# Output projections: the second half reads its weights' remainders from DRAM, and its squares follow the next weights' casts

## The chip, the cores and the metric

The kernel runs on one core of one Trainium2 chip. The metric is the device time of one execution in microseconds (us), the median over several runs.

## The reference

An encoder trunk of two layers over 1024 tokens of width 1024, in float32, one sequence. Layer 0 mixes with two parallel groups of heads (latent attention and stick-breaking attention), layer 1 with chunked band attention. Each mixer ends in one output projection and a residual add, and is followed by a SwiGLU feed-forward part (FFN):

```
for layer in range(2):
    u = rms_norm(h, g_mix[layer])
    o = heads of the mixer, concatenated           # (1024, 1024)
    h = h + o @ w_out[layer]                       # the output projection
    u = rms_norm(h, g_ffn[layer])
    h = h + (silu(u @ w_gate[layer]) * (u @ w_up[layer])) @ w_down[layer]
return rms_norm(h, g_final)
```

The sum of the squares of h over the 1024 features, one per token, is what the next `rms_norm` divides by.

## The kernel before, in words

**Numbers in two parts.** Matrix products are made from float32 operands split in two rounded parts: `hi` is the cast of x, `lo` the remainder x - hi. A product is three matmuls: `hi*hi`, `hi*lo`, `lo*hi` (`mm3`, lines 290 to 292). For weights the raw tile is called `wr` in the profile, the cast `wh` (on ACT, `round_to`, line 253) and the remainder `wl` (`rest`, line 258, on POOL or DVE). Each of the three has four buffers of 128x512, which is two weights, as one weight of the output projection is two such pieces.

**The output projection** works on features by tokens: two halves of 512 tokens (`hf` 0 and 1), in each eight output tiles `m` of 128 features. `out_half` makes one half. For a tile: load the residual two tiles ahead (`ld`), take the weight (two pieces, cast and remainder), eight k-steps of three matmuls into one PSUM bank (`mm`), add the residual on DVE (line 443), write the new h to DRAM (line 444), then square it on ACT and add the square to the running sum on DVE (`square_sum`, lines 305 to 314). Every half takes all eight weights, so each weight is loaded, cast and split twice per mixer.

**The first half** (`half(0)`) is woven into the attention of the last head pair. Its remainders are made by POOL. **The second half** is `half(1, 1)`: `early` is 1, the weights are cast and split one tile ahead, and their raw pieces are loaded one tile before that. Its remainders are made by DVE. It isn't run by the mixer: the mixer returns it as a generator, and `ffn` draws its steps as `rest`. The first tile runs before, the other seven within the pinned part (line 637): there PE, ACT, DVE and POOL keep the order in which the program issues their instructions, and the profile books all of them on line 77. SyncE, which issues all DMAs, isn't pinned: its order is made by the planner, by the times at which it thinks that data and buffers are ready. Between the k-steps of the second half, `ffn` issues work of its own: the norm of the first half (`blocks0`, from the matmul with `ones` that sums `s.acc[0]` over the partitions), the casts and remainders of the normed first half, and the loads, sums, casts and remainders of the FFN's first weights (`Pair`, `arrange`).

**After the second half** the FFN's products begin (`Seven`; `z` and `o` in PSUM). After the first product comes `blocks1`: the matmul with `ones` for `s.acc[1]`, the norm of the second half and the operands made from it.

Of the kernel before, what the change touches and what calls it, by code (L numbers as in the profile page):

```python
# [10 lines left out]
F32 = mybir.dt.float32  # L11
F32R = mybir.dt.float32r
AF = mybir.ActivationFunctionType
ALU = mybir.AluOpType
AX = mybir.AxisListType

P = 128
S = 1024
D = 1024
KD = D // P  # L20
HALF = 512
# [138 lines left out]
class Trunk:  # L160
# [113 lines left out]
            self.nc.sync.dma_start(tiles[-1][:, :w], src[:, c:c + w])  # L274
        return tiles

    def weight(self, src, n=1024, eng_hi="act", eng_lo="pool", into=None, raws=None):
        parts = []
        for c in range(0, n, HALF):
            w = min(HALF, n - c)  # L280
            raw = raws[c // HALF] if raws else self.raws(src[:, c:c + w], w)[0]
            hi, lo = into[c // HALF] if into else (self.wtile(0, "h", F32R), self.wtile(0, "l", F32R))
            self.split(raw[:, :w], hi[:, :w], lo[:, :w], eng_hi, eng_lo)
            parts.append((hi, lo))
        return Weight(parts)

# [138 lines left out]
                parts[k] = hi, lo  # L425
                yield

    def out_half(self, hf, w, parts, resid, ks, s, h_d, early=0):

        o = [x[0] for x in parts], [x[1] for x in parts]  # L430
        ahead, raws, wts = [], [], []
        for m in range(KD):
            while len(ahead) < min(AHEAD, KD - m):
                ahead.append(self.load(resid(hf, m + len(ahead))))
            x, h = ahead.pop(0), self.unit()
            for n in range(m + len(wts), min(m + early + 1, KD)):
                raw = raws.pop(0) if raws else None
                wts.append(self.weight(w[n], eng_lo="dve" if early else "pool", raws=raw))
            if early and m + early + 1 < KD:
                raws.append(self.raws(w[m + early + 1]))  # L440
            ps = self.bank()
            yield from self.dense(ps, wts.pop(0), o, ks)
            self.nc.vector.tensor_tensor(h, ps, x, ALU.add)
            self.nc.sync.dma_start(h_d[hf][m], h)
            s.h[hf].append(h)
            s.acc[hf] = self.square_sum(s.acc[hf], h)

    def parted(self, t):

# [804 lines left out]
    def free(self, gen):  # L1254

        for _ in gen:
            yield 0.0

    def ending(self, gen):
        yield from gen  # L1260
        self.flush()

    def mixer0(self, h_d):
        nc, a = self.nc, self.a
        o_d = self.spill("o0_")
        out = Stream()
        ks = [4, 5, 6, 7, 0, 1, 2, 3]
        half = lambda hf, *e: self.out_half(hf, a["w_out0"], o_p[hf], lambda hf, m: a["x"][hf, m], ks, out, h_d, *e)
        with self.phase("mix0", MIX0_TEMPS):
            self.load_consts()  # L1270
            vts = [[] for _ in range(4)]
            proj = ([[], []], [[], []], [])
            u = self.start(vts[0:2], proj)
            vgen = lambda w, g, hf: self.values(w, u, 4, KD, 1, vts[2 * g:2 * g + 2], hf)
            raw = [[[], []], [[], []]]
            cq, ckv = Stream(), Stream()
            va = [[] for _ in range(4)]
            mla = ([[], []], [[], []])

            def prepare():  # L1280
                yield from self.mla_latent([0, 1, 2], u, raw)
                yield from self.with_max(self.mla_latent([3, 4], u, raw), self.mla_norm(0, raw, cq), 0, 4)
                for hf in range(2):
                    nc.vector.tensor_tensor(self.cs[hf], self.cs[hf], cq.r[hf], ALU.mult)
                queries = self.chain(*[self.mla_query(e, cq, mla[0][e], "f", (0, 1)) for e in range(2)])
                yield from self.with_max(queries, self.mla_norm(1, raw, ckv), 2, 2)
                yield from self.values([a["w_uv"][0]], ckv, 2, 2, 2, va, [0, 1])
                yield from self.mla_keys(0, ckv, mla[1], "f", (0, 1))
                yield from self.free(self.mla_max(0, mla))

            for p in range(4):
                nxt = ([[], []], [[], []], [])
                if p < 2:
                    vw = [a["w_vb"][2], a["w_vb"][3]]
                    fill, cost = self.chain(self.sb_project(p + 1, u, nxt), vgen(vw, 1, [p])), 31.0
                elif p == 2:
                    fill, cost = self.chain(self.sb_project(3, u, nxt), self.rope_key(u)), 31.0
                else:
                    fill, cost = prepare(), 73.0
                self.weave(self.ending(self.sb_attend(p, proj, vts[p], o_d)) if p == 3 else  # L1300
                           self.sb_attend(p, proj, vts[p], o_d), 9.24, fill, cost)
                proj = nxt
            for p in range(4):
                nxt = ([[], []], [[], []])
                first, second = (self.mla_attend(p, hf, mla, va[p], o_d) for hf in range(2))
                top = lambda hf: self.mla_max(hf, mla)
                if p < 3:
                    att = self.chain(self.with_max(first, top(1), 0), self.with_max(second, self.mla_max(0, nxt), 4))
                    fill, cost = self.mla_project(p + 1, cq, ckv, nxt), 13.0
                    if p == 2:  # L1310
                        fill, cost = self.mla_project(3, cq, ckv, nxt, "c", [0]), 8.0
                    self.weave(att, 7.0, fill, cost)
                else:
                    o_p = [[None] * KD, [None] * KD]
                    first = self.with_max(first, self.out_loads(o_d[0], 3, o_p[0]), 0)
                    second = self.with_max(second, self.out_loads(o_d[1], 3, o_p[1]), 0)
                    fill = self.chain(self.mla_project(3, cq, ckv, mla, "c", [1]), self.free(top(1)))
                    self.weave(self.ending(first), 2.5, fill, 4.0)
                    o_p[0][3] = o_d[0][3]
                    self.weave(self.ending(second), 6.5, half(0), 41.5)  # L1320
                    o_p[1][3] = o_d[1][3]
                mla = nxt
        return out, half(1, 1)

    def mixer1(self, u, h_d, h2_d):
        a = self.a
        o_d = self.spill("o1_")
        out = Stream()
        half = lambda hf, *e: self.out_half(hf, a["w_out1"], o_p[hf], lambda hf, m: h_d[hf][m], list(range(KD)), out,
                                            h2_d, *e)  # L1330
        with self.phase("band", BAND_TEMPS):
            vts = [[] for _ in range(8)]
# [10 lines left out]
            for p in range(8):  # L1343
# [17 lines left out]
                else:  # L1361
                    o_p = [[None] * KD, [None] * KD]
# [158 lines left out]
```

## Time and profile before

| | |
|---|---|
| median of 3 runs | 2534.04 us (2530.97 to 2535.76) |
| the profiled execution | 2536.2 us, span from first to last instruction 2534.4 us |
| busy: PE, DVE, ACT, POOL | 97%, 74%, 46%, 19% of the span |
| granted TensorE clock | 0.994 |
| DMA | 324.94 MB, mean 128 GB/s |
| w_out loads | 64 of 256 KB, median 3.0 us to landing |
| second half of mixer 0 and of mixer 1, about | 616 to 665 us, 1820 to 1869 us |

A row of a timeline gives start, duration, engine, line, operation, output<-inputs and count, and in brackets how long the engine stood idle before it and who ended that. A row of waits gives who waited for whom: total us, times, longest. A row of windows gives the length, and for PE, PEld (weight loads), DVE, ACT and POOL the busy us with the number of instructions, then the granted clock, the DMA engines' busy share and GB/s. "SPq" is SyncE's DMA queue. Matmuls overlap in the pipeline, so their starts tell more than their durations.

### The profile page before, as it was taken

The page shows a single profiled execution, that of the slowest core. Times are in us where ns is not written, and L with a number is a line of the kernel's source. Part 1 is how long each engine was busy: PE and PEld are TensorE (multiplying, and loading weights), DVE is VectorE, ACT ScalarE, POOL GpSimd, SP SyncE. Part 2 cuts the span into 40 slices and gives each one's busy share as a digit, 9 for nine tenths or more (in the row PEclk, how much of TensorE's full clock was granted, in tenths as well). Part 3 has the DMA queues.
Part 4 walks back from the last instruction along what each step waited for, and adds up shares of the span by engine and source line. Part 5 has one row for each costly group of instructions (what it writes and reads, how often), then busy time and mean ns, then how long its engine had stood idle before and what let it go on. Part 6 is the DMA issues. An engine that isn't in the chain of part 4 may idle for free.

```text
span 2534.4 us, 33597 instructions
## 1 busy us (share of the span) xinstructions
PE 2460.9 (97%) x11710; PEld 1934.4 (76%) x11710; DVE 1870.9 (74%) x3072; ACT 1155.3 (46%) x2004; POOL 493.7 (19%) x475
## 2 busy tenths in 40 slices
PE   9999989999999999999999999999999999999997
PEld 7776766667778888888877777776777888888886
DVE  7988796675886666677666777778688666667775
ACT  5777565443454444433253443444445443443324
POOL 0333335761000000000132333435200000000004
PEclk9999999999999999999999999999999999999999
DMA  5222102145344434576552222223633433447661
GB/s 156 55 65 65 38 22 73 51 122 178 108 137 141 146 108 142 172 259 221 205 170 69 83 84 79 76 90 106 197 119 129 145 136 113 146 160 260 217 210 71
DMA packets 182824, 324.94 MB, mean 128 GB/s; under 512 B 21376, under 2 KB 37632, under 8 KB 182656
## 3 DMA queue, kind: packets, MB, share of 16 engines
q1 hardware_dynamic: 182656, 322.81, 38.3%
q8 instruction: 92, 1.51, 0.3%
q14 instruction: 76, 0.62, 0.1%
HBM read 223.63 MB, written 84.41 MB: 122 GB/s over the span
## 4 chain that ended last, share of the span: by engine, by line
PE 71%; DVE 9%; DMA 2%; ACT 2%; issue 1%; POOL 1%; DVEq 0%; POOLq 0%; SPq 0%; ACTq 0%
PE z L77 25%; PE mm L77 12%; PE o L77 7%; PE mm L290 6%; PE mm L291 5%; PE mm L292 5%; PE o L850 3%; DVE u L77 2%; PE z L1230 1%; PE z L1231 1%; PE z L1204 1%; DVE u L313 1%; PE z L1149 1%; PE o L1114 1%; PE z L1074 1%
## 5 line engine op out<-in xcount | busy, mean ns | idle before, releaser
L77 PE MATMUL z<-u,wh 128*128 128x512 f32 x976 | 302.2, 390 | 6.5 <-DVE u L77 6.5
L77 PE MATMUL z<-u,vh 128*128 128x512 f32 x976 | 302.8, 392 | 2.2 <-DVE u L77 2.2
L290 PE MATMUL mm<-u,wh 128*128 128x512 f32 x720 | 287.7, 400 | 3.3 <-DVE u L724 1.6
L291 PE MATMUL mm<-u,wh 128*128 128x512 f32 x720 | 283.6, 394 | 1.4 <-DVE u L258 1.4
L292 PE MATMUL mm<-u,wl 128*128 128x512 f32 x720 | 283.5, 394 | 0.0
L258 POOL TENSOR_TENSOR wl<-wr,wh 128x512 fp32r<-128x512 f32 (+2 forms) x95 | 121.5, 1283 | 785.1 <-ACT wh L253 726.2
L77 PE MATMUL mm<-u,wh 128*128 128x512 f32 x720 | 223.4, 392 | 4.6 <-ACT wh L77 4.6
L77 PEld LDWEIGHTS z<-u,wh 128*128 128x128 f32 x976 | 183.1, 188 | 47.3 <-DVE u L77 9.5
L77 PEld LDWEIGHTS z<-u,vh 128*128 128x128 f32 x976 | 183.8, 189 | 42.9 <-ACT u L77 3.1
L77 PE MATMUL z<-u,vl 128*128 128x512 f32 x488 | 190.7, 391 | 0.0
L77 PE MATMUL z<-u,wl 128*128 128x512 f32 x488 | 190.0, 389 | 0.6 <-DVE wl L77 0.6
L290 PEld LDWEIGHTS mm<-u,wh 128*128 128x128 f32 x720 | 135.6, 188 | 50.8 <-issue 23.5
L77 PEld LDWEIGHTS mm<-u,wh 128*128 128x128 f32 x720 | 134.7, 188 | 35.7 <-ACT wh L77 6.9
L292 PEld LDWEIGHTS mm<-u,wl 128*128 128x128 f32 x720 | 135.5, 188 | 29.2 <-issue 1.7
L291 PEld LDWEIGHTS mm<-u,wh 128*128 128x128 f32 x720 | 135.6, 188 | 27.3 <-DVE u L258 2.0
L77 PE MATMUL mm<-u,vh 128*128 128x512 f32 x496 | 152.7, 389 | 0.0
L77 PE MATMUL mm<-u,wl 128*128 128x512 f32 x360 | 140.8, 391 | 0.8 <-DVE wl L77 0.5
L258 POOL TENSOR_TENSOR u<-wr,u 128x512 fp32r<-128x512 f32 x8 | 10.9, 1372 | 670.2 <-ACT u L253 670.2
L850 PE MATMUL o<-a,u 128*64 128x512 f32 (+3 forms) x768 | 139.2, 474 | 0.5 <-DVE f L1122 0.4
L1097 POOL TENSOR_TENSOR b<-b,a 128x512 f32<-128x512 f32 (+3 forms) x80 | 109.2, 1365 | 122.9 <-ACT a L1233 99.5
L77 ACT CAST vh<-vr 128x512 fp32r<-128x512 f32 (+1 forms) x166 | 95.9, 578 | 81.7 <-DVE vr L77 30.8
L1233 ACT ACTIVATE a<-a 128x1024 f32<-128x1024 f32 (+3 forms) x96 | 70.0, 737 | 129.7 <-DVE a L1232 128.8
(244 smaller groups left out, 5874.1 us busy)
## 6 DMA issues: line engine op xcount, KB each, us to landing
u<-f_t SPq DMA_DIRECT2D x144, 256.0 KB, 5.0
vr<-in_w_up SPq DMA_DIRECT2D x88, 256.0 KB, 4.4
wr<-in_w_gate SPq DMA_DIRECT2D x88, 256.0 KB, 3.6
f_t<-x SPq DMA_DIRECT2D x72, 256.0 KB, 2.0
wr<-in_w_out SPq DMA_DIRECT2D x64, 256.0 KB, 3.0
f_t<-e SPq DMA_DIRECT2D x54, 256.0 KB, 3.7
ld<-f SPq DMA_DIRECT2D x54, 256.0 KB, 5.0
u<-u SPq DMA_DIRECT2D x96, 128.0 KB, 2.2
```

What stands on the lines that cost most here:

```text
L77: return lambda *a, **k: self.tc.keep_in_program_order(f(*a, **k))
L258: self.eng(eng).tensor_tensor(lo, src, hi.bitcast(F32), ALU.subtract)
L290: mm(out, wh, xh, start=first, stop=False, skip_group_check=onto)
L291: mm(out, wh, xl, start=False, stop=False, skip_group_check=onto)
L292: mm(out, wl, xh, start=False, stop=last, skip_group_check=onto)
L313: self.eng(eng).tensor_tensor(acc, acc, sq, ALU.add)
L850: return self.nc.tensor.matmul(o[rh, cs], vt[j // 4][:, j % 4, rh], w[:, e, cs], start=first, stop=last)
L1074: nc.tensor.matmul(z[:, e, :n], qs[e][hf][0][0:kr, r * P:(r + 1) * P], ks[e][kh][0][0:kr, :n], start=True, stop=True)
L1097: self.eng("dve" if dest[2] else "pool").tensor_tensor(st["esum"][:, :, cs], old[:, :, cs], ex[:, :, cs], ALU.add)
L1114: return nc.tensor.matmul(den[64 * e:64 * e + 64, :], self.ones[:, 0:64], esum[:, e, :], start=True, stop=True)
L1149: mm(z[:, e, cs], kth[0:kr, bs], qh[0:kr, cs], start=True, stop=False)
L1233: nc.scalar.activation(ex[:, :, cs], ex[:, :, cs], AF.Exp)
```

## The change

In the first half, each remainder that POOL has made is also written to a DRAM tile (`w_d`, 16 tiles of 256 KB for each mixer). In the second half, `weight` still loads the raw piece and casts it on ACT, but loads the remainder from DRAM instead of having DVE subtract. Besides, in tiles 1 to 7 of the second half, the square of the tile before no longer follows its residual add: ACT's square is issued after the second k-step (behind the casts of the next weight), and DVE adds it to the sum after the fifth. The last tile is squared as before.

```diff
-    def weight(self, src, n=1024, eng_hi="act", eng_lo="pool", into=None, raws=None):
+    def weight(self, src, n=1024, eng_hi="act", eng_lo="pool", into=None, raws=None, los=None):
...
-            self.split(raw[:, :w], hi[:, :w], lo[:, :w], eng_hi, eng_lo)
+            if los:
+                self.round_to(eng_hi, hi[:, :w], raw[:, :w])
+                self.nc.sync.dma_start(lo.bitcast(F32), los[c // HALF])
+            else:
+                self.split(raw[:, :w], hi[:, :w], lo[:, :w], eng_hi, eng_lo)
...
-    def out_half(self, hf, w, parts, resid, ks, s, h_d, early=0):
+    def out_half(self, hf, w, w_d, parts, resid, ks, s, h_d, early=0):
...
+        def add_square():
+            if s.acc[hf] is None:
+                s.acc[hf] = sq
+            else:
+                self.nc.vector.tensor_tensor(s.acc[hf], s.acc[hf], sq, ALU.add)
...
-                wts.append(self.weight(w[n], eng_lo="dve" if early else "pool", raws=raw))
+                wts.append(self.weight(w[n], raws=raw, los=w_d[n] if early else None))
+                if not early:
+                    for (_, lo), d in zip(wts[-1].parts, w_d[n]):
+                        self.nc.sync.dma_start(d, lo.bitcast(F32))
...
-            yield from self.dense(ps, wts.pop(0), o, ks)
+            for k, us in enumerate(self.dense(ps, wts.pop(0), o, ks)):
+                if early and m and k == 1:
+                    sq = self.unit()
+                    self.nc.scalar.square(sq, s.h[hf][-1])
+                if early and m and k == 4:
+                    add_square()
+                yield us
...
-            s.acc[hf] = self.square_sum(s.acc[hf], h)
+            if not early or m == KD - 1:
+                s.acc[hf] = self.square_sum(s.acc[hf], h)
...
+    def remainders(self, name):
+        return [[self.dp.tile([P, HALF], F32, name=f"{name}{m}_{c}") for c in range(2)] for m in range(KD)]
```

`mixer0` and `mixer1` make the tiles (`self.remainders("w0_")`, `self.remainders("w1_")`) and pass them to `out_half`.

More of the change, by code (lines that the diff above doesn't have):

```diff
@@ L426, in out_loads @@
                 yield
-    def out_half(self, hf, w, parts, resid, ks, s, h_d, early=0):
+    def out_half(self, hf, w, w_d, parts, resid, ks, s, h_d, early=0):
         o = [x[0] for x in parts], [x[1] for x in parts]
-        ahead, raws, wts = [], [], []
+        ahead, raws, wts, sq = [], [], [], None
+        def add_square():
[3 more added lines that the diff above has]
+                self.nc.vector.tensor_tensor(s.acc[hf], s.acc[hf], sq, ALU.add)
         for m in range(KD):
@@ L1264, in mixer0 @@
         nc, a = self.nc, self.a
-        o_d = self.spill("o0_")
+        o_d, w_d = self.spill("o0_"), self.remainders("w0_")
         out = Stream()
         ks = [4, 5, 6, 7, 0, 1, 2, 3]
-        half = lambda hf, *e: self.out_half(hf, a["w_out0"], o_p[hf], lambda hf, m: a["x"][hf, m], ks, out, h_d, *e)
+        half = lambda hf, *e: self.out_half(hf, a["w_out0"], w_d, o_p[hf], lambda hf, m: a["x"][hf, m], ks, out, h_d, *e)
         with self.phase("mix0", MIX0_TEMPS):
@@ L1326, in mixer1 @@
         a = self.a
-        o_d = self.spill("o1_")
+        o_d, w_d = self.spill("o1_"), self.remainders("w1_")
         out = Stream()
-        half = lambda hf, *e: self.out_half(hf, a["w_out1"], o_p[hf], lambda hf, m: h_d[hf][m], list(range(KD)), out,
+        half = lambda hf, *e: self.out_half(hf, a["w_out1"], w_d, o_p[hf], lambda hf, m: h_d[hf][m], list(range(KD)), out,
                                             h2_d, *e)
```

## The prediction

> **What bounds the kernel now.** I read the page first, then the PE's waits in the two stretches that the change touches, then the timelines of PE, DVE, ACT and SyncE there. The page:
>
> ```profile
> span 2534.4 us, 33597 instructions
> PE 71%; DVE 9%; DMA 2%; ACT 2%; issue 1%; POOL 1%; DVEq 0%; POOLq 0%; SPq 0%; ACTq 0%
> ```
>
> PE carries the chain that ends last, so time is won only where PE waits. The change touches the output projections: their first halves (about 505 to 622 us and 1715 to 1828 us) and their second halves, which run inside the FFN's pinned order up to the matmul with `ones` (`o<-u,ones`) that sums the squares of the second half. The PE's waits in the two second halves, mixer 0 (622 to 668.6 us), then mixer 1 (1828 to 1874.4 us); columns: total us, times, longest:
>
> ```profile
> PE mm L77 <- ACT wh L77: 2.4, 3, 1.3
> PE o L77 <- DVE u L77: 0.5, 1, 0.5
> ...
> PE mm L77 <- ACT wh L77: 2.2, 2, 1.4
> PE o L77 <- DVE u L77: 1.3, 1, 1.3
> PE z L77 <- DVE wl L77: 0.6, 1, 0.6
> ```
>
> PE waits for ACT's casts of w_out and for DVE. What that costs in full is read from the starts of matmuls in PE's timeline (start us, us):
>
> ```profile
> 627.93 0.61 PE L77 MATMUL mm<-u,wh 128*128 128x512 f32 x2
> 633.37 0.62 PE L77 MATMUL mm<-u,wh 128*128 128x512 f32 x2
> ...
> 644.76 0.73 PE L77 MATMUL mm<-u,wh 128*128 128x512 f32 x2 [0.35 <-ACT wh L77]
> 652.28 0.73 PE L77 MATMUL mm<-u,wh 128*128 128x512 f32 x2 [1.34 <-ACT wh L77]
> 659.15 0.74 PE L77 MATMUL mm<-u,wh 128*128 128x512 f32 x2 [0.69 <-ACT wh L77]
> 668.56 1.12 PE L77 MATMUL o<-u,ones 128*128 128x512 f32 x2 [0.49 <-DVE u L77]
> 1832.60 0.61 PE L77 MATMUL mm<-u,wh 128*128 128x512 f32 x2
> 1874.35 1.12 PE L77 MATMUL o<-u,ones 128*128 128x512 f32 x2 [1.31 <-DVE u L77]
> ```
>
> 627.93 is the start of output tile m=2 and 633.37 that of m=3: a tile is 8 k-steps of three matmuls and takes 5.44 us undisturbed, 0.68 us a step. From m=2 to `ones` lie six tiles and the four steps of the FFN's first product: 6 x 5.44 + 4 x 0.68 = 35.36 us. They took 668.56 - 627.93 = 40.63 us and 1874.35 - 1832.60 = 41.75 us. So PE loses 5.27 us in mixer 0 and 6.39 us in mixer 1, 11.66 us together: all there is to win in these two stretches.
>
> Why ACT's casts are late is seen in one tile (m=4), DVE rows, then ACT rows:
>
> ```profile
> 642.33 0.68 DVE L77 TENSOR_TENSOR u<-mm,ld 128x512 f32<-128x512 f32 x1
> 643.71 0.69 DVE L77 TENSOR_TENSOR u<-u,u 128x512 f32<-128x512 f32 x1 [0.70 <-ACT u L77]
> 644.32 1.28 DVE L77 TENSOR_TENSOR wl<-wr,wh 128x512 fp32r<-128x512 f32 x2
> 645.52 0.74 DVE L77 SCALAR_TENSOR_TENSOR u<-u,gains,u 128x512 f32<-128x512 f32 x1
> 649.86 0.68 DVE L77 TENSOR_TENSOR u<-mm,ld 128x512 f32<-128x512 f32 x1
> 666.43 0.68 DVE L77 TENSOR_TENSOR u<-mm,ld 128x512 f32<-128x512 f32 x1
> ...
> 643.04 0.63 ACT L77 ACTIVATE u<-u 128x512 f32<-128x512 f32 x1 [1.19 <-DVE u L77]
> 643.58 1.12 ACT L77 CAST wh<-wr 128x512 fp32r<-128x512 f32 x2
> ```
>
> DVE adds the residual of m=3 at 642.33, though PE had finished that tile at the start of m=4 (633.37 + 5.44 = 638.81): DVE is 3.5 us behind. ACT's square waits for that add, the casts for m=5 stand behind the square in ACT's queue, and PE gets them at 644.76. From this add to the next (649.86) DVE takes 7.53 us, 2.09 more than PE's tile. DVE's work per tile is what bounds this stretch.
>
> **The change part by part.** (1) Removed from DVE: two remainders (`wl<-wr,wh`) a tile. Their slot runs from 644.32 to 645.52: 1.20 us. (2) Square behind the casts: DVE no longer idles for ACT's square between residual add and sum; the sum comes at k=4 and costs its slot, the idle 0.70 us goes (643.71 - 642.33 = 1.38, less a slot of 0.61 = 0.77 with its edges). Together 1.97 us: the fullest tile falls to 7.53 - 1.97 = 5.56 us against PE's 5.44. That 0.1 us is caught up in the next tile: the window's sum shows it,
>
> ```profile
> core 0: us, PE busy (x) PEld busy (x) DVE busy (x) ACT busy (x) POOL busy (x), PEclk, DMA share, GB/s
> 627.93:668.56 40.63, 37.26 (x157) 28.63 (x155) 35.58 (x58) 19.65 (x35) 0.00 (x0) 1.00 0.59 201
> ```
>
> DVE's 35.58 us less five pairs of remainders (5 x 1.28) is 29.2 us in the 35.36 us that PE needs. ACT is busy 19.65 us and gets nothing new; its casts now wait only for a free `wh` buffer, that is for the end of the tile before, and have 5.44 us for 1.12 us of work. So I cost parts 1 and 2 at the whole PE loss of m=2 to m=7. (3) The end of the stretch: the last residual add, square, sum and `ones` took 668.56 - 666.43 = 2.13 us; now the add can start when the last tile ends, and the four steps beside it last 4 x 0.68 = 2.72 us. So this wait goes too, and with it the wait in mixer 1 for the FFN's first remainder (0.6 us). Gain of 1 to 3: 11.66 us. Everything behind `ones` depends on it and moves with it; the waits there stay:
>
> ```profile
> 668.56:720.00 51.44, 48.17 (x206) 38.30 (x207) 46.18 (x73) 25.89 (x45) 0.00 (x0) 1.00 0.12 37
> PE z L77 <- DVE u L77: 3.3, 3, 2.0
> ```
>
> (4) Added in the first half: 16 writes of 256 KB a mixer on SyncE's queue, each waiting for POOL's remainder, with residual loads, operand loads and the next w_out loads behind it. SyncE's own waits from 505 to 622 us:
>
> ```profile
> SPq L274 <- POOL wl L258: 47.6, 17, 10.8
> ```
>
> The queue already stands 47.6 us waiting for the same POOL results, since the next w_out load takes the buffer that this remainder sets free. A write that waits for the same event adds its issue time (under 0.5 us: two take 0.93 in a row below) to a queue that mostly stands; PE gets its weights a tile ahead. Cost 0; between -2 and +2 us, the size of PE's few waits there, since the order of SyncE's queue is the planner's:
>
> ```profile
> PE z L1149 <- ACT a L1152: 1.7, 1, 1.7
> PE mm L291 <- DVE u L258: 1.2, 1, 1.2
> ```
>
> POOL keeps its remainders; a `wl` buffer is now also held by the write, but PE reads it only after that.
>
> (5) Added in the second half: 16 loads of 256 KB a mixer. For tile m+1 the load needs a `wl` buffer that PE frees at the end of m-1, which is the start of m; PE wants the data at the third matmul of m+1, 5.44 + 0.45 = 5.9 us later. This is the new wait, and what is queued behind it on SyncE are the row write of h, the residual load and the next w_out loads. Its price hangs on landing. SyncE's rows in m=2; then landing of w_out loads (median us) issued 621 to 634 us and 634 to 646 us; then the DMA load of m=1 and m=2 in mixer 0 and in mixer 1:
>
> ```profile
> 629.78 0.33 SPq L444 DMA_DIRECT2D h<-u  x1
> 630.15 0.43 SPq L192 DMA_DIRECT2D ld<-in_x  x1
> 631.77 0.93 SPq L274 DMA_DIRECT2D wr<-in_w_out  x2
> ...
> wr<-in_w_out SPq DMA_DIRECT2D x4, 256.0 KB, 4.3
> wr<-in_w_out SPq DMA_DIRECT2D x4, 256.0 KB, 2.8
> ...
> 621.58:627.93 6.35, 6.35 (x28) 4.88 (x27) 4.34 (x7) 2.98 (x5) 0.00 (x0) 1.00 0.77 246
> 627.93:633.37 5.44, 5.44 (x26) 4.50 (x25) 4.70 (x8) 2.60 (x5) 0.00 (x0) 1.00 1.04 378
> 1826.26:1832.60 6.34, 6.34 (x27) 4.88 (x26) 4.34 (x7) 2.98 (x5) 0.00 (x0) 1.00 0.82 266
> 1832.60:1838.04 5.44, 5.44 (x25) 4.50 (x24) 4.71 (x8) 2.58 (x5) 0.00 (x0) 1.00 0.87 287
> ```
>
> In most tiles the second load, issued 0.9 us into the tile and landing in 2.8, is there at 3.7 of 5.9 us; even behind h and the residual load (an add of 0.69 us, then four issues of 0.37 to 0.47: at about 2.1) at 4.9. Tight are m=1 and m=2, where the FFN's first weights are fetched. Mixer 0 moved 246 x 6.35 + 378 x 5.44 = 3.62 MB there; four more loads make 4.67 MB in 11.79 us, 396 GB/s, over the 378 that the fullest row shows: 0.55 us late. Mixer 1: 3.25 + 1.05 = 4.30 MB in 11.78 us, 365 GB/s: it fits. So I take 0.6 us for part 5. Its bounds: 0 (the remainders go ahead of the others) and 6 us: behind h and the residual load, second issue at 631.0, landing 4.3, there at 635.3 where 633.8 is wanted, 1.5 us, for two tiles in two mixers.
>
> The Trainium skill, "DMA: Bandwidth & Descriptors", Specifications, speaks against this part: it gives about 358 GB/s from HBM for a core. By it the same bytes would be an estimated 1.25 us late in mixer 0 and 0.2 us in mixer 1, and the sum would be 0.9 us less gain. The row with 378 GB/s stands above that figure, so the measurement decides.
>
> Sum: -11.66 + 0.6 = -11.1 us. The profiled execution took 2536.2 us, 2.2 over the median of 2534.04; the gain is taken from either: 2525.1, and against the median 2523.0 us.
>
> **The rivals.** A, above: 2523, its own range 2520.5 to 2527. B, the remainders come late in the crowded tiles (the planner puts them behind h, or the DMA queue is full): up to 6 us of the gain are given back, 2527 to 2532. For it: 1.04 DMA share in m=2. Against it: the remainder is ready to load before h, whose write waits for DVE's add. C, the gain is swallowed behind `ones`: DVE is busy 46.18 of 51.44 us there and PE waits 3.3 us for it; if DVE's work there did not move forward with `ones`, PE would stand that much longer and the time would stay at 2534. Against it: that work begins with the result of `ones`. D, slower: every remainder lands late, in all 12 tiles that are loaded inside the FFN, because SyncE's queue holds it behind h and the residual load (issue at 2.1) and the added traffic makes each landing as bad as 5.8 us: 7.9 - 5.9 = 2.0 us x 12 = 24, less 11.7: 2546. It decides from 0.97 us a tile (11.66 / 12). Against it: 2.8 us landing outside the crowded tiles.
>
> **How the numbers follow.** A 0.60, B 0.20, C 0.12, D 0.08. Forecast 2523.0. The range 2520 to 2530.5 holds A and most of B and leaves C and D out. A measurement of this kernel tells about 0.2% (5.1 us) from no change. Faster: A and half of B, 0.70; same: the rest of B and most of C, 0.21; slower: D and a rest, 0.09.
>
> **What the profile of the changed kernel would show.** Right: `wl<-wr,wh` on DVE six pairs fewer in each stretch; ACT's casts at the start of each tile and the square behind them; six tiles at 5.44 us in a row; m=2 to `ones` in about 35.4 to 36 us; the same 3.3 us of waits behind. Wrong: PE waiting for a DMA into `wl` (B, D), at the third matmul of a tile; stalls behind `ones` grown by the 5 us (C); PE waits in the first half that were not there, with SyncE standing before a remainder's write.

## The result, and the profile after

| | before | after |
|---|---|---|
| median (lowest to highest) | 2535.54 us (2530.97 to 2539.75) | 2523.43 us (2519.2 to 2527.14) |
| ratio | | 0.9949, 95% interval 0.9939 to 0.9959 |
| span of the profiled execution | 2534.4 us | 2521.8 us |

The change makes the kernel 12 us faster on the medians; by the ratio it is 0.51%, and the whole interval lies below 1. PE's share of the chain that ended last rose from 71% to 74%, DVE's fell from 9% to 7%:

```profile
span 2521.8 us, 33700 instructions
PE 74%; DVE 7%; DMA 2%; ACT 1%; issue 1%; POOL 0%; DVEq 0%; SPq 0%; POOLq 0%; ACTq 0%
```

The PE's waits in the second half of mixer 0 (622 to 664.2 us), then right behind its `ones` (664.2 to 724 us). In mixer 1 (1822 to 1862 us) there is none left:

```profile
PE o L77 <- DVE u L77: 0.2, 1, 0.2
...
PE z L77 <- DVE u L77: 3.2, 3, 2.0
```

In PE's timeline, the first matmuls of tiles m=2 to m=7, of the FFN's first product, and `ones`; then m=2 and `ones` of mixer 1:

```profile
628.33 0.61 PE L77 MATMUL mm<-u,wh 128*128 128x512 f32 x2
633.76 0.61 PE L77 MATMUL mm<-u,wh 128*128 128x512 f32 x2
639.21 0.61 PE L77 MATMUL mm<-u,wh 128*128 128x512 f32 x2
644.64 0.61 PE L77 MATMUL mm<-u,wh 128*128 128x512 f32 x2
650.09 0.61 PE L77 MATMUL mm<-u,wh 128*128 128x512 f32 x2
655.52 0.61 PE L77 MATMUL mm<-u,wh 128*128 128x512 f32 x2
660.97 0.61 PE L77 MATMUL z<-u,wh 128*128 128x512 f32 x2
664.09 1.12 PE L77 MATMUL o<-u,ones 128*128 128x512 f32 x2 [0.25 <-DVE u L77]
...
1826.44 0.61 PE L77 MATMUL mm<-u,wh 128*128 128x512 f32 x2
1861.80 1.02 PE L77 MATMUL o<-u,ones 128*128 128x512 f32 x2
```

Six tiles of 5.44 us stand in a row. From m=2 to `ones` it is 664.09 - 628.33 = 35.76 us and 1861.80 - 1826.44 = 35.36 us, where 40.63 and 41.75 stood before. The windows of these two stretches:

```profile
628.33:664.09 35.76, 35.52 (x157) 29.09 (x155) 29.36 (x48) 19.32 (x35) 0.00 (x0) 1.00 0.87 301
1826.44:1861.80 35.36, 35.36 (x157) 29.28 (x156) 29.73 (x48) 18.85 (x34) 0.00 (x0) 1.00 0.88 304
```

DVE is busy 29.36 us with 48 instructions instead of 35.58 us with 58: five pairs of remainders went (six pairs over the whole second half, as foretold). In their place the DMA engines, at a share of 0.59 before, are now at 0.87.

Where the 12.6 us of span came from: 4.87 us in mixer 0's stretch and 6.39 us in mixer 1's, 11.26 together. Another 1.69 us was won between the two, which no step of the prediction had: a wait in the last products of layer 0's FFN, here before and after, shrank (the order there is the planner's, and it fell out otherwise). Up to the first stretch 0.40 us was lost. A second profile does not bear out these last two: in e9, the same kernel, the wait is 0.2 us as well, but the part between the stretches took 2.65 us longer than here, and the part ahead of them 2.66 us less. Only the gain in the stretches repeats.

```profile
PE mm L290 <- DVE u L724: 1.6, 1, 1.6
...
PE mm L295 <- DVE u L747: 0.2, 1, 0.2
```

### The profile page after: what moved, and what is told of

The parts are those of the page before. It is cut to its first block, busy times and chain, and to the rows that moved or that the text cites. A ratio compares the mean times of both kernels' runs of the same rounds, so it can differ in the third digit from the quotient of the medians.

```text
span 2521.8 us, 33700 instructions
## 1 busy us (share of the span) xinstructions
PE 2456.9 (97%) x11710; PEld 1936.0 (77%) x11710; DVE 1849.5 (73%) x3040; ACT 1156.1 (46%) x2004; POOL 495.1 (20%) x475
## 4 chain that ended last, share of the span: by engine, by line
PE 74%; DVE 7%; DMA 2%; ACT 1%; issue 1%; POOL 0%; DVEq 0%; SPq 0%; POOLq 0%; ACTq 0%
PE z L77 25%; PE mm L77 14%; PE o L77 7%; PE mm L295 6%; PE mm L296 6%; PE mm L297 6%; PE o L873 3%; DVE u L77 2%; PE z L1253 1%; PE z L1254 1%; PE z L1227 1%; DVE u L318 1%; PE z L1172 1%; PE o L1137 1%; PE z L1097 1%
## 5 line engine op out<-in xcount | busy, mean ns | idle before, releaser
L77 ACT CAST wh<-wr 128x512 fp32r<-128x512 f32 (+1 forms) x190 | 110.5, 584 | 49.4 <-DVE wr L77 29.3
```

Of the source, the lines that this page charges most:

```text
L77: return lambda *a, **k: self.tc.keep_in_program_order(f(*a, **k))
```

## Experiments

The stretch from the `ones` of the first half's sum to the `ones` of the second half's takes 39.66 us when PE never waits in it. What each kernel lost over that, in the profiled execution, and its time:

| kernel | lost, mixer 0 / mixer 1 (us) | median (us) | ratio to before, 95% interval |
|---|---|---|---|
| before | 5.28 / 6.39 | 2535.54 | |
| the change | 0.41 / 0 | 2523.43 | 0.9949 [0.9939, 0.9959] |
| e1 remainders only | 2.70 / 1.17 | 2526.53 | 0.9965 [0.9954, 0.9977] |
| e2 squares only | 2.58 / 3.68 | 2533.1 | 0.9992 [0.9983, 1.0001] |
| e3 writes only | 5.09 / 5.12 | 2532.88 | 0.9992 [0.9984, 1.0001] |
| e4 POOL makes remainders | 5.30 / 5.85 | 2537.81 | 1.0012 [1.0003, 1.0021] |
| e5 remainders only, gate apart | 0.01 / 0.01 | 2522.3 | 0.9954 [0.994, 0.9967] |
| e6 remainders loaded twice | 7.76 / 8.86 | 2540.59 | 1.0025 [1.0014, 1.0036] |
| e7 change, gate apart | 0.47 / 0.01 | 2524.04 | 0.9958 [0.9944, 0.9971] |
| e8 squares only, gate apart | 1.74 / 1.74 | 2527.44 | 0.997 [0.9959, 0.998] |
| e9 the change, profiled again | 0 / 0.01 | 2522.76 (one time) | |
| e10 squares only, profiled again | 1.81 / 3.47 | 2530.35 (one time) | |

The kernel before had 2535.95 us beside e1 to e4, 2534.8 us beside e5 to e8 and 2537.6 us beside e9 and e10.

**e1: the remainders come from DRAM, the squares stay where they were.**

```diff
-            for k, us in enumerate(self.dense(ps, wts.pop(0), o, ks)):
-                ...
+            yield from self.dense(ps, wts.pop(0), o, ks)
...
-            if not early or m == KD - 1:
-                s.acc[hf] = self.square_sum(s.acc[hf], h)
+            s.acc[hf] = self.square_sum(s.acc[hf], h)
```

> Remainders go through DRAM as in the change; squares stay where they were, ahead of the next weights' casts. Theory 1 (the loss was DVE's lag; what takes enough work off DVE cures it): DVE needs 1.20 us less a tile, its lag stays under 1.5 us, the casts end at most 2.4 us after the residual add and PE does not wait. m=2 to the matmul with ones takes 35.4 to 36.2 us in both mixers, time 2523 to 2525. Theory 2 (the order in ACT's queue was the cause, the casts wait behind a square that waits for DVE): about half of the loss stays, 38 us and more in each mixer, 2529 or more.

It gained 9.4 us on the median and left 2.70 and 1.17 us in the stretches, its time between what its two theories said. What was left looks like DVE's doing in the PE's waits of mixer 0, but DVE itself had stood for a DMA (second fence: DVE's timeline, where it adds two loaded pieces of the FFN's first gate weight, `w_gate`; third: SyncE's queue):

```profile
PE o L77 <- DVE u L77: 1.4, 1, 1.4
PE z L77 <- DVE wl L77: 0.8, 1, 0.8
```

```profile
658.39 0.69 DVE L77 TENSOR_TENSOR s<-wr,wr 128x512 f32<-128x512 f32 x1 [3.19 <-DMA wr<-in_w_gate]
```

```profile
650.66 1.11 SPq L103 DMA_DIRECT2D e<-in_w_gate  x1
651.87 0.87 SPq L103 DMA_DIRECT2D wr<-in_w_gate  x2
```

The FFN's first weights borrow the `wr` buffers of the projection. A cast that comes later frees its buffer later, SyncE puts other loads (`e`) ahead, and the two gate pieces are issued at 651.87, 30.6 us behind the first half's `ones`; in the change the last of them is issued 28.0 us behind it (651.98 - 624.02). DVE, in pinned order, stands 3.19 us for them, and the last residual add and its square stand behind. That raised a new theory: the order on ACT matters only through this buffer. e5 tests it.

**e2: the squares behind the casts, the remainders on DVE, nothing written or read.**

```diff
-                wts.append(self.weight(w[n], raws=raw, los=w_d[n] if early else None))
-                if not early:
-                    ... (the writes)
+                wts.append(self.weight(w[n], eng_lo="dve" if early else "pool", raws=raw))
```

> Only the squares are moved behind the casts; DVE makes the remainders of the second half as before, nothing goes through DRAM. Theory 1 (lag): DVE saves only the 0.77 us of idle time a tile, its slots are 5.6, 6.2, 6.8 and 6.1 us in tiles 2 to 5 against PE's 5.44, the lag grows to about 2.8 us, but the casts no longer hang on it and the remainders come 1.9 us after the residual add, just in time; only the sum before ones comes late: 35.6 to 36.8 us in both mixers, 2524 to 2526. Theory 3 (DVE's throughput, so that only the remainders' removal can cure it): the tiles stay bound by DVE, 38 us and more in each mixer, 2529 or more. If e1 and e2 both come near the change, either part alone does it and the DRAM traffic was not needed.

It removed 2.7 us from each stretch, under half of the loss, which is nearer to its Theory 3 than to Theory 1. On the median it can't be told from before. DVE still comes late (waits of PE, then DVE's timeline):

```profile
PE o L77 <- DVE u L77: 1.7, 1, 1.7
```

```profile
658.16 0.69 DVE L77 TENSOR_TENSOR s<-wr,wr 128x512 f32<-128x512 f32 x1 [1.45 <-DMA wr<-in_w_gate]
```

Here too a `w_gate` piece is part of it, 1.45 us; how much is for e8. In e10, the same kernel profiled again, 1.81 and 3.47 us were lost, so the stretches repeat to within 0.8 us. The time shows less than the stretches: 2.9 us by the medians, 2.0 by the ratio, of 5.4. An estimate from the granted clock accounts for most of that gap: its mean was 0.9930 over the eleven runs of e2 and 0.9938 over the 28 of before, and 0.0008 of 2535 us is 2 us. In the profiled execution of e2 the clock fell to half behind the wait at `ones` in mixer 1, which costs 1.7 us (last section); in e10 it did not, and there the span is 5.8 us under that of before, where the stretches gained 6.4.

> Squares only once more, for a second profile. In the first the stretches gained 5.4 us and the time only about 2 us, with three windows of 0.93 clock (700, 1850 and 1900 us) where the kernel before had two. If the missing 3.4 us are the clock's, the windows differ here and span and stretches agree better; if they belong to the kernel, the same windows and about the same span (2530) come again.

**e3: the first half writes its remainders, and nobody reads them.** Against e1:

```diff
-                wts.append(self.weight(w[n], raws=raw, los=w_d[n] if early else None))
+                wts.append(self.weight(w[n], eng_lo="dve" if early else "pool", raws=raw))
```

> Only the writes of the first half's remainders to DRAM are added to the kernel before; nothing reads them, DVE makes the second half's remainders, squares as before. Theory (the writes are free, SyncE's queue already stands for the same POOL results): 2534 to 2537, m=2 to ones 40.6 and 41.7 us as before, no new PE waits in the first halves. Rival (the writes hold up the queue): the first halves grow by 1 to 4 us, 2537 to 2540.

0.9992, with 1 in the interval: 32 writes of 256 KB cost nothing that shows. The PE's wait for casts is the one of before, and the one wait of the first half for a remainder's operand keeps its size:

```profile
PE mm L77 <- ACT wh L77: 2.4, 3, 1.4
...
PE mm L296 <- DVE u L258: 1.2, 1, 1.2
```

**e4: e2, but POOL makes the remainders of the second half, where it was idle.**

```diff
-                wts.append(self.weight(w[n], eng_lo="dve" if early else "pool", raws=raw))
+                wts.append(self.weight(w[n], raws=raw))
```

> Squares moved; the second half's remainders are made by POOL, which has nothing to do there, instead of coming from DRAM. Theory 1: same relief of DVE as the change, remainders there 3.3 us after the start of a tile where 5.9 are wanted, no new traffic: 35.4 to 36 us in both mixers, 2522 to 2525. Rival (POOL and DVE hinder each other at two-input operations on the same memory): DVE's operations beside POOL's last longer than 0.69 us, its lag comes back and the stretches are 1 us or more longer than with DRAM, 2526 or more.

DVE lost the same instructions as in the change, without a byte more of DMA, and nothing was won, as the rival said: the ratio is 1.0012, and the stretches lost 5.30 and 5.85 us where 5.28 and 6.39 stood. POOL's remainders (the tile's group: shortest, median and longest in ns), two instructions of DVE beside one of them, and the window:

```profile
L77 POOL TENSOR_TENSOR wl<-wr,wh x10: 1294/1724/1767, 629.4 to 653.7; 128x512 fp32r<-128x512 f32 x10
```

```profile
652.04 3.36 POOL L77 TENSOR_TENSOR wl<-wr,wh 128x512 fp32r<-128x512 f32 x2 [0.65 <-ACT wh L77]
...
651.86 0.68 DVE L77 TENSOR_TENSOR s<-s,vr 128x512 f32<-128x512 f32 x1
652.46 1.78 DVE L77 TENSOR_TENSOR vl<-vr,vh 128x512 fp32r<-128x512 f32 x1
```

```profile
626.00:668.00 42.00, 37.97 (x162) 29.84 (x161) 39.24 (x49) 19.34 (x35) 16.20 (x10) 1.00 0.59 193
```

While POOL subtracts, a DVE instruction of 0.68 us can take 1.2 to 1.78 us: 49 instructions keep DVE busy for 39.24 us, where 48 took 29.36 us in the change. PE waits for both:

```profile
PE mm L77 <- POOL wl L77: 1.6, 2, 1.3
PE mm L77 <- DVE u L77: 1.2, 1, 1.2
```

The Trainium skill, "SBUF — State Buffer", section "SBUF: two separate sides", says that DVE with two inputs from SBUF and GpSimd share a pair of ports that only one of them holds at a time; this trace agrees, with 1.78 us for 0.68.

**e5, e7, e8: e1, the change and e2, with two of the gate pieces in buffers of their own.** Pieces "21" and "22" of the first gate weight no longer take the projection's `wr` buffers; nothing else differs. The kernel before was not run in this way. There DVE stands for no gate piece in mixer 0 and 1.2 us for one in mixer 1, so by the trace these buffers are at most a small part of its loss.

```diff
                     for x in ("11", "12", "21", "22"):
-                        after[lead[x]].append(lambda x=x, pair=pair: pair.load(x))
+                        role = "x" if t == 0 and x in ("21", "22") else None
+                        after[lead[x]].append(lambda x=x, pair=pair, role=role: pair.load(x, role))
```

> As e1 (remainders through DRAM, squares in their old place), and two of the FFN's first w_gate pieces (21 and 22 of the first pair) are loaded into tiles of their own instead of waiting for the buffers of w_out's raw pieces. In e1 DVE stood 3.2 us for their landing, and PE lost 2.70 us in mixer 0 and 1.17 us in mixer 1 between the two matmuls with ones against the undisturbed 39.66 us. Theory (that landing is all that e1 lacks; the order of ACT's queue costs nothing once DVE keeps up): 39.7 to 40.2 us in both mixers, 2522 to 2525. Rival (the casts behind the square still cost): 41 us or more in mixer 0, 2525 to 2528.

e5 loses 0.01 us in either stretch and is at 2522.3 us, with an interval that overlaps the one of the change almost wholly. Its square still stands ahead of the casts and DVE still idles for it (DVE's timeline), and yet PE runs through (its `ones`, 661.94 - 622.27 = 39.67 us):

```profile
655.37 0.69 DVE L77 TENSOR_TENSOR u<-u,u 128x512 f32<-128x512 f32 x1 [0.70 <-ACT u L77]
655.97 0.69 DVE L77 TENSOR_TENSOR s<-x,x 128x512 f32<-128x512 f32 x1
```

```profile
622.27 1.02 PE L77 MATMUL o<-u,ones 128*128 128x512 f32 x2
661.94 1.02 PE L77 MATMUL o<-u,ones 128*128 128x512 f32 x2
```

So the theory that ACT's order makes the casts late falls for the kernel with the remainders gone: the order costs nothing there, and the 2.70 and 1.17 us that e1 kept hung on the gate pieces.

> As e2 (only the squares moved, remainders by DVE), with the two w_gate pieces in tiles of their own. In e2 PE lost 2.58 us and 3.68 us between the matmuls with ones; DVE was 3 us behind PE by tile 6 and then stood 1.45 us for a w_gate piece. Theory (two causes in a row: DVE's lag and the landing): the landing goes, 1 to 1.5 us in each mixer, the lag stays: 41 to 41.8 us, and a time 2 to 3 us under e2's 2533. Rival (the lag alone sets the end): as e2, 42 us and more.

e8 keeps 1.74 us in each stretch, as its theory said, and gains 7.4 us, which is more than it said and 0.6 of the change's, without a remainder in DRAM. Against e2 and e10 the gate pieces in time were worth 0.1 to 0.8 us in mixer 0 and 1.7 to 1.9 us in mixer 1. What remains is DVE's work itself: from m=2 to `ones` (first row) it is busy 35.11 of 37.09 us, as much as PE needs undisturbed, and `ones` waits for its last sum of squares:

```profile
625.14:662.23 37.09, 35.95 (x157) 28.94 (x155) 35.11 (x58) 19.57 (x35) 0.00 (x0) 1.00 0.68 234
```

```profile
PE o L77 <- DVE u L77: 0.8, 1, 0.8
...
PE o L77 <- DVE u L77: 1.4, 1, 1.4
```

> The change, with the two w_gate pieces in tiles of their own as in e5. Theory: the last 0.4 us that PE loses in mixer 0 goes (DVE stood 1.8 us for that landing): 39.66 to 39.8 us in both mixers, 2522 to 2524.5, not to be told from the change. Rival (the planner then issues these loads into the crowded tiles 1 and 2, ahead of remainders): PE waits of 0.5 to 2 us there, 2524 to 2527.

e7 can't be told from the change, nor from e5: with the remainders loaded and the gate pieces in time, PE's waits are nearly used up, whichever way the squares stand. Its theory held in mixer 1 alone: the 0.47 us in mixer 0 were a remainder that landed late (first fence: waits of PE's weight loads), as its rival said, at the low end of its range. The only other such wait outside e6 is one of 0.3 us in e1. The change's 0.41 us there had 0.25 at `ones`, behind a gate piece for which DVE stood 1.80 us; in e9 DVE stood 0.21 us for it, and nothing was lost:

```profile
PEld mm L77 <- DMA wl<-w: 0.6, 1, 0.6
```

```profile
658.22 0.69 DVE L77 TENSOR_TENSOR s<-wr,wr 128x512 f32<-128x512 f32 x1 [1.80 <-DMA wr<-in_w_gate]
```

> The change once more, for a second profile. The first showed the TensorE clock at 0.93 and 0.97 in two windows of 25 us (1900 to 1925 us, 2475 to 2500 us), other kernels in other windows. If these windows belong to the kernel, they are in the same places again; if they come by chance, the stretches between the matmuls with ones are 40.07 and 39.66 us again and the windows elsewhere.

The stretches took 39.66 and 39.67 us. Of the two falls of the clock, the one near 2500 us came again (2499.7 us after 2498.7); the one in 1900 to 1925 us did not, and the clock fell at 704 us instead.

**e6: the change, and each remainder of tiles 2 to 7 loaded a second time, into a buffer that nobody reads.**

```diff
+                for c in range(2 if early and n > 1 else 0):
+                    self.nc.sync.dma_start(self.tmp("x"), w_d[n][c])
```

> The change, and each remainder of tiles 2 to 7 is loaded a second time, into a tile that nothing reads: 12 more loads of 256 KB in each mixer inside the FFN's first stretch, just behind the real ones. Theory (the loads have slack outside the crowded tiles 1 and 2, and there it is used up): there, 4 loads more make 5.7 MB in 11.8 us, 485 GB/s where 390 is the most seen, so tile 3's remainder and the w_gate pieces come late: ones to ones 41 to 44 us in both mixers instead of 40.07 and 39.66, 2526 to 2532. Rival (SyncE's queue and the DMA engines have room to spare): under 40.5 us in both, 2522 to 2525.

It is 17 us slower than the change, of which 7.35 and 8.86 us lie in the stretches; these took 47.42 and 48.52 us, more than even its theory said. PE now waits for the remainders (waits in mixer 0, then mixer 1):

```profile
PE mm L77 <- DMA wl<-w: 4.9, 4, 2.1
...
PE mm L77 <- DMA wl<-w: 4.4, 3, 2.7
```

These are 9.3 of the 16.2 us. About 5 us more are the clock's, by an estimate: its mean was 0.96 and 0.93 over the two stretches (0.04 x 47.4 + 0.07 x 48.5), where the change has 1.00.

The DMA engines are a little fuller (the window below, against 0.87 and 301 in the change), but the remainders hardly land later: 4.9 us in the median in mixer 0 in both kernels, 4.3 us in the change and 4.5 us in e6 in mixer 1.

```profile
622.00:668.59 46.59, 41.66 (x173) 32.98 (x171) 32.28 (x51) 20.32 (x36) 0.00 (x0) 0.96 0.90 317
```

SyncE's order, however, turned: in the change the two pieces of a tile are issued half a tile apart (first four rows), ahead of h as soon as the earlier piece is done with; in e6 they come as a pair behind the write of h, which waits for DVE's add, and behind the residual load (last three rows):

```profile
636.68 0.33 SPq L286 DMA_DIRECT2D wl<-w  x1
639.40 0.33 SPq L286 DMA_DIRECT2D wl<-w  x1
642.12 0.33 SPq L286 DMA_DIRECT2D wl<-w  x1
644.84 0.33 SPq L286 DMA_DIRECT2D wl<-w  x1
```

```profile
639.88 0.33 SPq L468 DMA_DIRECT2D h<-u  x1
640.26 0.42 SPq L192 DMA_DIRECT2D ld<-in_x  x1
640.77 0.87 SPq L286 DMA_DIRECT2D wl<-w  x2
```

By these rows and the landings the place in the queue weighs more than the fuller engines; how the 17 us divide between the two was not measured.

## Why the prediction was right, point by point

**The bound and the size (steps 1 and 2).** PE's loss between m=2 and `ones` was all there was to win in these stretches, and 11.26 of the 11.66 us came: 4.87 of 5.27, 6.39 of 6.39. That gain is no luck: e9 gives it all but 0.01 us. That the forecast, 2523.0 us, lies 0.4 us from the median is partly luck. It was taken from the median of three runs, 2534.04; from the 2535.54 of seven the same 11.1 us would have given 2524.4. And in the profiled execution 0.4 us kept in mixer 0 and 0.40 us lost ahead of the stretch stand against 1.69 us won in between, which was not foreseen and did not repeat.

**How the two parts share it.** Here the working was too strict. It took the fullest tile, 7.53 us of DVE, and needed both 1.20 us of remainders and 0.77 us of idling to bring it to 5.56. By that, e1 would have stayed at 7.53 - 1.20 = 6.33 us in a full tile. e5 shows that the remainders alone do it, once the gate pieces are in time. What decides, by e5 and e8, is DVE's sum over the stretch, which the prediction quoted too: 30.03 us of work in 35.36 us (e5) leaves 5 us for idling; 35.11 us (e8) leaves next to none. The squares, moved alone and with the gate pieces in time (e8), win two thirds of the loss in mixer 0 (5.28 to 1.74) but end on that sum. So the parts are not terms of a sum; each takes most of the same loss.

**The end of the stretch (step 3).** The last add, square and sum did fit behind the four steps, but for 0.25 us in mixer 0, and there because DVE stood 1.80 us for the gate piece. The wait for the FFN's first remainder in mixer 1 went too. What the prediction missed is the gate pieces: they use the same `wr` buffers, and the moved casts set when they can be loaded. With the remainders gone, this was the one real use of moving the squares, as e1 and e5 show.

**The waits behind `ones`** stayed, 3.2 us for 3.3, and rival C is out.

**The writes (step 4)** cost 0 as said: e3.

**The loads (step 5)** were taken at 0.6 us and cost nothing that shows. The step that was wrong is where the buffer comes free. The prediction let both pieces wait for the end of m-1; the issues above lie 2.72 us apart, half a tile, since each piece's buffer comes free when its own four k-steps are over. The first piece of m=5 is issued at 636.68 and wanted at 644.64 + 0.45 = 645.1: 8.4 us, where 5.9 were reckoned. Against landings of 2.7 to 6.0 us in mixer 0, 4.9 in the median, that is cover enough. The overload in m=1 and m=2 didn't come either, since less of the traffic fell there (mixer 0, m=1 and m=2 of the change):

```profile
621.97:628.33 6.36, 6.36 (x28) 4.88 (x27) 3.05 (x5) 2.56 (x4) 0.00 (x0) 1.00 0.85 264
628.33:633.76 5.43, 5.43 (x25) 4.50 (x24) 5.00 (x9) 3.79 (x8) 0.00 (x0) 1.00 0.91 290
```

264 x 6.36 + 290 x 5.43 = 3.25 MB moved, where 4.67 were put; part of it came later, m=3 and m=4 ran at 364 and 359 GB/s. Nor are the 378 GB/s of the fullest row a limit, as the prediction took them: in layer 0's FFN of the kernel before, from 1075 to 1110 us, the DMA engines moved 396 GB/s for 35 us, and by that the 396 GB/s of its sum would have fitted. The Trainium skill's 358 GB/s ("DMA: Bandwidth & Descriptors", Specifications) would have made the loads an estimated 1.25 us late in mixer 0. No load of m=1 and m=2 was late, and the 396 GB/s over 35 us stand above that figure too.

**Rivals B and D.** The argument against B, that a remainder is ready before the write of h, held, and e6 shows what it was worth: with the order turned and more traffic, the stretches took 16.2 us more, which is more than the change wins. D's mechanism was real. Its break-even of 0.97 us a tile was passed there only with the clock's part: 16.2 / 12 = 1.35 us a tile in all, 9.3 / 12 = 0.78 us by PE's waits for remainders alone.

**One sign was off:** not all casts stood at a tile's start. The two of m=4 waited for their raw pieces, 1.12 us (ACT's timeline, below) and 0.63 us, and were still in time:

```profile
639.87 0.62 ACT L77 CAST wh<-wr 128x512 fp32r<-128x512 f32 x1 [1.12 <-DMA wr<-in_w_out]
```

## What to carry to other kernels

Where an engine beside PE is late in every tile, compare its sum over the stretch with PE's before counting one tile: if the sum fits, taking away one of several causes may win nearly everything, and the parts' gains do not add up. Follow every buffer that a moved instruction sets free to the load that takes it next, even if that load belongs to another stage. Work moved from an engine to the DMA queue holds as long as the queue issues it ahead of what waits; the same loads, with others added and behind a waiting write, cost more here than the work did.

## What the runs showed of the hardware that was not expected

DVE and POOL slowed each other: with POOL subtracting 128x512 tiles beside it (e4), DVE took up to 1.78 us for 0.68, and POOL 1.72 us in the median where its shortest took 1.29.

A wait of PE can cost more than its length. Behind `ones`, in both mixers, PE waits 2.04 us for DVE in every kernel. Behind 14 of these 24 waits (two in each of the twelve profiles) the granted clock falls to half for 3.4 us, behind the others it doesn't. Windows of before in mixer 1 (the wait, then from 1 us behind it on), and of e8 behind the same wait of 2.04 us:

```profile
1915.06:1917.10 2.04, 0.00 (x1) 0.00 (x1) 2.04 (x5) 1.20 (x3) 0.00 (x0) 1.00 0.47 128
1918.16:1921.55 3.39, 3.39 (x10) 2.68 (x9) 3.29 (x7) 1.15 (x2) 0.00 (x0) 0.51 0.00 0
...
1905.15:1910.00 4.85, 4.85 (x21) 4.02 (x22) 4.75 (x8) 1.71 (x4) 0.00 (x0) 1.00 0.00 0
```

At half clock, 3.39 us lose 1.7 us. The Trainium skill, "TensorE: Matmul & The Clock Gate", section "What's actually happening", has the clock set by windows of 3.4 us that run freely, half after an idle one; the length agrees with 3.39 us and the free running with the chance in it, but here 2.04 us of idling were enough.

The trace's record of the granted clock shows what decides it. In each profile the half-clock stretches begin whole multiples of 3.41 us apart (in before 1918.06 and 2511.98 us, 174 times 3.413). With time divided into windows on that grid, in the 14 cases one window held 1.91 us or more of the wait, and the next one ran at half clock; in the other ten an edge parted the wait, and no window held more than 1.86 us of it. So where the wait falls on the grid, which differs from one execution to the next, decides.

In e2 the wait of 1.96 us at `ones` of mixer 1 did it too, a wait that the change hasn't got; in e10, the same kernel, an edge parted the wait of 1.94 us into 1.22 and 0.72, and the clock stayed. The window of e2:

```profile
1865.00:1870.00 5.00, 3.04 (x8) 1.49 (x7) 2.31 (x4) 1.79 (x3) 0.00 (x0) 0.78 0.28 103
```

So one profiled execution against another is good to a few us of span, and stretches between two named instructions carry the argument better.
